# First half of the feed-forward as seven products over halves of K, tokens and gate/up

## The chip, the core and the metric

The kernel runs on one core of one Trainium2 chip. A core has five engines that run side by side, each from its own queue: TensorE (PE, matrix products into PSUM, with its weight loads listed as PEld), VectorE (DVE), ScalarE (ACT), GpSimd (POOL) and SyncE (SP), whose queue here issues the DMAs. The metric is the time on the device in microseconds, from launch to end; smaller is better.

## The reference

Two layers of a diffusion trunk, for 128 context tokens (`x_prompt`) and 1024 latent tokens (`x_sample`) that share one set of weights. Each layer is a mixer (layer 0 latent attention beside gated linear attention, layer 1 differential attention) and a dense SwiGLU feed-forward, each between two RMS norms and scaled by adaLN vectors. All is float32. The change touches the feed-forward and what stands around it:

```python
def trunk_layer(x, li, cond, P, rope, ctx):
    mod = (jax.nn.silu(cond) @ P['w_mod'][li] + P['b_mod'][li])[:, None, :]
    shift1, scale1, gate1, shift2, scale2, gate2 = jnp.split(mod, 6, axis=-1)
    g = P['g_norm'][li]
    ...
    x = x + gate1 * rms_norm(out, g[1])
    h = rms_norm(x, g[2]) * (1.0 + scale2) + shift2
    gate, up = jnp.split(h @ P['w_ffn_in'][li], 2, axis=-1)
    f = (jax.nn.silu(gate) * up) @ P['w_ffn_out'][li]
    x = x + gate2 * rms_norm(f, g[3])
```

The model width is 1024, the hidden width 2816, so `w_ffn_in` is 1024 x 5632 (gate columns, then up columns) and `w_ffn_out` 2816 x 1024.

## The kernel before

**Order.** The program isn't written in the order in which it runs. A `Recorder` (line 171) takes down every operation with its data dependences, and `schedule` (line 327) places them by a list schedule: a cost model gives each operation a duration, and an engine takes the ready operation that can start first, among several the one recorded first. Operations recorded with `copy`, `tt` or `scaled` (lines 635 to 650) may go to one of two or three engines, and the schedule chooses. `issue` (line 504) then emits the operations in that order, each engine working through its own in sequence. All instructions are emitted at line 539, so the profile tells them apart by tile, not by line.

**Memory.** SBUF is cut into named blocks (lines 587 to 591: nine `bU` of 12 KB a partition, four `bW` of 9, six `bE` of 4.5, four `bC` of 3, one `bH` of 9, two `bst` of 4), and tile classes are lists of slots in these blocks (lines 593 to 616). A slot can be given to a tile of one class only when no earlier recorded tile of another class that shares the block is still to be placed. The profile names a tile by its block (U, W, E, C, H, st).

**Products.** A float32 operand is split into a high part, rounded to the type that TensorE takes at full rate (`F32R`), and a remainder, and a product is three matmuls: high by high, high by remainder, remainder by high (`mm3`, line 807).

**First half of the feed-forward** (`ffn_in`, line 1530). The normed input h lies in SBUF transposed, in three groups of 384 tokens (`groups`, line 1367), high parts and remainders. For each of 22 hidden tiles of 128, `load_w` fetches a gate and an up weight (1024 x 128 each) and splits them; for each group `dense_m` makes the two products, ScalarE takes Silu of the gate and VectorE multiplies by the up. The result goes to DRAM (`hid_d`), and for each pair of tiles four sums of token halves go to `hs_d`.

**Second half, and the mixers' output projections** (`project`, line 1428). These are already Strassen products of Winograd's form over latent tokens: seven products of 512 columns ("12", "11", S2, S1, S3, "22", S4 on the left), each looping over pairs j of K tiles: 11 for `w_ffn_out`, 4 for the mixers' outputs. Rows of weights stay in classes `Wr1`, `Wr2` or `Wo`; left operands come from DRAM through class `Ss`; split operands stand in class `k4`.

**Between them** (`finish`, line 1370). `fin(t, parts)` takes a finished block of 128 tokens: norm, gate, add to x, store; and, where another sub-layer follows, the next norm, eight transposes, the adaLN scale and shift, and the split into h. It takes three tiles of 4 KB a partition per block from class `fx`, which has five slots. Block 0 is the context's; it is finished after the second product, blocks 5 to 8 after X and Y are complete, 1 to 4 after the last product.

**adaLN vectors** (`mod_vectors`, line 753). Ten of the twelve vector sets are made on VectorE, 8 passes a set, 80 in all. A pass loads four tiles of `w_mod` (class `M`, two slots), multiplies and adds them into a tile `ma`, transposes and reduces. `beside(n, after)` (line 947) records the next n passes at that point, ready once the operation `after` is done. Before the change 26 are recorded in layer 0's input projections and the rest in layer 0's `ffn_in`, three for each hidden tile until none is left. `diff_qk` (line 1595) makes layer 1's queries and keys from h, tile by tile, and turns them by rotary tables.

## Time and profile before

| | before |
|---|---|
| median of 3 runs | 3533.42 us (3529.42 to 3538.25) |
| the profiled execution's own time | 3530.54 us |
| its span, first to last instruction | 3528.7 us |
| mean granted TensorE clock | 0.967 |
| busy: TensorE, VectorE, ScalarE, GpSimd | 94%, 64%, 38%, 26% of the span |
| moved by DMA | 480.98 MB, 136 GB/s |

Busy time is an average over stages with different limits, so the tables of stretches further down say more than these shares. In the lists of instructions a row gives start, duration, engine, operation, output tile and input tiles, shapes, how many were merged, and in brackets the idle time before it and what ended that. Matmuls are pipelined: the records of two in a row overlap, so the cost of one in a run is the run's length by its count, not a record's own length.

### The profile page before, as it was taken

The page shows a single profiled execution, that of the slowest core. Times are in us where ns is not written, and L with a number is a line of the kernel's source. Part 1 is how long each engine was busy: PE and PEld are TensorE (multiplying, and loading weights), DVE is VectorE, ACT ScalarE, POOL GpSimd, SP SyncE. Part 2 cuts the span into 40 slices and gives each one's busy share as a digit, 9 for nine tenths or more (in the row PEclk, how much of TensorE's full clock was granted, in tenths as well). Part 3 has the DMA queues.
Part 4 walks back from the last instruction along what each step waited for, and adds up shares of the span by engine and source line. Part 5 has one row for each costly group of instructions (what it writes and reads, how often), then busy time and mean ns, then how long its engine had stood idle before and what let it go on. Part 6 is the DMA issues. An engine that isn't in the chain of part 4 may idle for free.

```text
span 3528.7 us, 52056 instructions
## 1 busy us (share of the span) xinstructions
PE 3325.8 (94%) x18525; PEld 3018.3 (86%) x18525; DVE 2256.5 (64%) x5656; ACT 1332.9 (38%) x2558; POOL 933.3 (26%) x858
## 2 busy tenths in 40 slices
...
GB/s 198 141 183 168 170 158 186 109 121 127 151 155 133 161 140 135 147 176 97 90 136 167 198 123 135 139 142 144 78 144 149 105 94 80 99 80 144 109 87 156
DMA packets 433345, 480.98 MB, mean 136 GB/s; under 512 B 38463, under 2 KB 343166, under 8 KB 432414
## 3 DMA queue, kind: packets, MB, share of 16 engines
...
## 4 chain that ended last, share of the span: by engine, by line
PE 53%; DVE 7%; DMA 6%; POOL 3%; issue 2%; ACT 1%; SPq 0%; DVEq 0%; POOLq 0%; ACTq 0%
PE psum L539 53%; DMA M<-in_w_mod 3%; DVE ma L539 2%; POOL E L539 2%; DMA U<-v_d 1%; DVE U L539 1%; DVE E L539 1%; POOL sm L539 1%; ACT E L539 1%; DVE W L539 0%; DVE H L539 0%; DMA U<-in_w_ffn_out 0%; DMA U<-k_d 0%; ACT U L539 0%; DVE C L539 0%
## 5 line engine op out<-in xcount | busy, mean ns | idle before, releaser
L539 PE MATMUL psum<-U,W 128*128 128x384 f32 (+1 forms) x7674 | 1369.9, 337 | 19.8 <-ACT U L539 12.0
L539 PEld LDWEIGHTS psum<-U,W 128*128 128x128 f32 x7674 | 1334.6, 189 | 30.7 <-ACT U L539 13.4
L539 PE MATMUL psum<-E,E 128*128 128x512 f32 x2520 | 589.1, 393 | 17.6 <-DVE E L539 8.4
L539 PEld LDWEIGHTS psum<-E,E 128*128 128x128 f32 x2520 | 470.2, 188 | 129.1 <-DVE E L539 20.3
L539 ACT ACTIVATE E<-psum 128x384 f32<-128x384 f32 (+4 forms) x197 | 98.9, 504 | 944.7 <-PE psum L539 938.1
L539 DVE SCALAR_TENSOR_TENSOR ma<-M,sc,ma 128x128 f32<-128x128 f32 x1120 | 345.3, 372 | 102.6 <-DMA M<-in_w_mod 101.7
L539 PE MATMUL psum<-U,U 128*128 128x384 f32 (+4 forms) x1630 | 328.1, 341 | 4.4 <-DVE E L539 2.3
L539 ACT ACTIVATE E<-E,sm 128x1152 f32<-128x1152 f32 (+1 forms) x248 | 288.1, 1168 | 114.2 <-DVE sm L539 93.3
L539 DVE TENSOR_SCALAR_CACHE_REDUCE E<-psum 128x384 f32<-128x384 f32 (+1 forms) x600 | 303.8, 541 | 33.0 <-PE psum L539 16.0
L539 PE MATMUL psum<-W,U 128*128 128x256 f32 (+2 forms) x1616 | 311.7, 340 | 11.2 <-DVE W L539 3.1
L539 DVE TENSOR_TENSOR E<-E,psum 128x384 f32<-128x384 f32 (+1 forms) x148 | 82.0, 555 | 353.7 <-PE psum L539 353.5
L539 PEld LDWEIGHTS psum<-W,U 128*128 128x128 f32 x1616 | 258.9, 195 | 44.9 <-DVE W L539 5.0
L539 ACT ACTIVATE E<-C 128x512 fp32r<-128x512 f32 (+1 forms) x303 | 181.8, 628 | 285.7 <-PE psum L539 216.6
L539 PEld LDWEIGHTS psum<-U,U 128*128 128x128 f32 (+1 forms) x1630 | 265.3, 191 | 18.6 <-DVE E L539 10.0
L539 DVE TENSOR_TENSOR E<-C,E 128x512 fp32r<-128x512 f32 (+2 forms) x257 | 201.1, 786 | 117.1 <-ACT E L539 111.6
L539 PE MATMUL psum<-U,H 128*128 128x384 f32 x1368 | 247.1, 335 | 0.0
L539 PEld LDWEIGHTS psum<-U,H 128*128 128x128 f32 x1368 | 237.6, 188 | 0.2
L539 DVE TENSOR_TENSOR W<-st,W 128x1024 fp32r<-128x1024 f32 (+3 forms) x111 | 138.3, 1247 | 114.4 <-ACT W L539 112.7
L539 POOL TENSOR_TENSOR E<-C,E 128x512 fp32r<-128x512 f32 (+2 forms) x102 | 131.2, 1287 | 255.8 <-ACT E L539 186.8
L539 PE MATMUL psum<-ident,E 128*128 128x128 f32 x1241 | 175.2, 280 | 20.3 <-POOL E L539 8.1
L539 POOL TENSOR_TENSOR E<-E,E 128x1152 f32<-128x1152 f32 (+2 forms) x74 | 179.0, 2422 | 52.0 <-ACT E L539 26.7
L539 POOL TENSOR_TENSOR sm<-sm,mhalf 128x1 f32<-128x1 f32 (+2 forms) x124 | 93.3, 754 | 342.7 <-DVE sm L539 335.7
...
## 6 DMA issues: line engine op xcount, KB each, us to landing
...
hs_d<-U SPq DMA_DIRECT2D x88, 256.0 KB, 4.0
C<-hs_d SPq DMA_DIRECT2D x88, 256.0 KB, 2.6
...
C<-hid_d SPq DMA_DIRECT2D x66, 256.0 KB, 2.7
```

Source lines behind the costliest of these rows:

```text
L539: getattr(self.real[e], m)(*[res(a) for a in args], **{n: res(a) for n, a in kw.items()})
```

## The change

`ffn_in` handles two hidden tiles (256 gate and 256 up columns) at a time and takes the latent tokens' product as a 2 x 2 by 2 x 2 block product: weights A[r, c], r gate or up, c the half of K (512 rows each); tokens by half of K and half of the 1024 latent tokens. It is done with seven products ("21", "11", T2, T3, T1, T4, "22"), each of two column tiles, four K tiles and 512 tokens. Products that add up stay in the same PSUM tiles. The context tokens' products are made beside, with the tokens as the stationary operand and 256 weight columns moving.

The token side of the seven products is made once, in `fin`: an object `Halves` takes each finished block f (`put`), splits its halves and their sums to high part and remainder and keeps them in SBUF. Blocks 5 to 8 come first; they are stored in DRAM and read back when block 1 to 4 is finished, since the sums need both. The sub-layer that feeds layer 1's mixer keeps the old groups of 384 tokens (`Groups`).

The slots of `Wo` move, `fin` takes its tiles from `fz` or `fy` where `Halves` is the target, and there are new classes for the kept sums, the weights and the temporaries. The passes of `mod_vectors` are spread anew: 23 in layer 0's `ffn_in`, 12 in the products S2 and S1 of its `project`, the rest in `diff_qk`; a pass's first multiplications are recorded with `scaled`.

```diff
-            ("Wo", inside(bU[6:8] + bU[5:6], 4, 3), None), ("Wr1", inside(bU[0:4], 4, 3), None), ("Wr2", inside(bU[4:8], 4, 3), None),
+            ("Wo", inside(bU[4:7], 4, 3), None), ("Wr1", inside(bU[0:4], 4, 3), None), ("Wr2", inside(bU[4:8], 4, 3), None),
             ("F2", inside(bW[0:3], 2, 4) + inside(bE[5:6], 2, 2), None), ("Ss", [(a, a + 2) for a, _ in bC], None),
-            ("k4", [(a, a + 4) for a, _ in bE[0:5]], None), ("fx", inside(bU[8:9], 4, 3) + inside(bH, 4, 2), None), ("Fs", inside(bU[8:9], 2, 6), None),
+            ("k4", [(a, a + 4) for a, _ in bE[0:5]], None), ("fx", inside(bU[8:9], 4, 3) + inside(bH, 4, 2), None),
+            ("Ta", inside(bU[0:4], 4, 3), None), ("Tb", inside(bU[4:8], 4, 3), None),
+            ("Tc", inside(bH, 4, 2) + inside(bU[8:9], 4, 3) + inside(bst[0:1], 4, 1), None),
+            ("fz", inside(bU[7:9], 4, 3), None), ("fy", [(a, a + 4) for a, _ in bE[0:5]] + inside(bst[1:2], 4, 1), None),
+            ("As", [(a, a + 4) for a, _ in bE], None), ("Wb", inside(bW[0:3], 4, 2), None),
+            ("tq", inside(bW[3:4], 2, 4) + [(a, a + 2) for a, _ in bC] + inside(bst[1:2], 2, 2), None),
...
-                        dve.tensor_scalar(out=acc[:, j], in0=st[:, 0, :], scalar1=s, scalar2=None, op0=ALU.mult)
+                        scaled(acc[:, j], st[:, 0, :], s)
...
-    def groups():
-        return [[R.tile("Uh", [128, KD, GW], F32R) for j in range(2)] for g in range(NG)]
+    class Halves:
+        def __init__(self, name):
+            self.name, self.T, self.hc = name, {}, None
+            self.kept = [dtile([128, KD, 128], f"{name}_{q}") for q in range(4)]
+        def split(self, i, q, src):
+            if i not in self.T:
+                cls = {"22": "Ta", "T3": "Ta", "T1": "Ta", "T4": "Tc"}.get(i, "Tb")
+                self.T[i] = [[R.tile(cls, [128, 2, 512], F32R) for _ in range(2)] for _ in range(2)]
+            c = slice(q * 128, (q + 1) * 128)
+            for kp in range(2):
+                hi, lo = [self.T[i][j][kp][:, :, c] for j in range(2)]
+                part = src[:, 2 * kp:2 * kp + 2]
+                copy(hi, part)
+                tt(lo, part, hi, ALU.subtract)
+        def put(self, t, f):
+            a, b = f[:, 0:4], f[:, 4:8]
+            if t == 0:
+                self.hc = [R.tile("Tc", [128, KD, 128], F32R) for _ in range(2)]
+                copy(self.hc[0], f)
+                tt(self.hc[1], f, self.hc[0], ALU.subtract)
+            elif t > 4:
+                self.split("22", t - 5, b)
+                tt(b, b, a, ALU.subtract)
+                self.split("T3", t - 5, b)
+                sp.dma_start(out=self.kept[t - 5], in_=f)
+            else:
+                q = t - 1
+                o = R.tile("fy", [128, KD, 128])
+                sp.dma_start(out=o, in_=self.kept[q])
+                self.split("21", q, b)
+                self.split("11", q, a)
+                tt(o[:, 4:8], o[:, 4:8], a, ALU.add)
+                self.split("T2", q, o[:, 4:8])
+                tt(o[:, 0:4], o[:, 0:4], a, ALU.subtract)
+                self.split("T1", q, o[:, 0:4])
+                tt(b, b, o[:, 4:8], ALU.subtract)
+                self.split("T4", q, b)
+    class Groups:
+        def __init__(self):
+            self.h = [[R.tile("Uh", [128, KD, GW], F32R) for j in range(2)] for g in range(NG)]
+        def put(self, t, f):
+            g, c0 = divmod(t * 128, GW)
+            hi, lo = [v[:, :, c0:c0 + 128] for v in self.h[g]]
+            copy(hi, f)
+            tt(lo, f, hi, ALU.subtract)
...
-            xt, tm = R.tile("fx", [128, D]), R.tile("fx", [128, D])
+            cls = "fx" if not isinstance(h, Halves) else "fy" if 1 <= t <= 4 else "fz"
+            xt, tm = R.tile(cls, [128, D]), R.tile(cls, [128, D])
...
-            u = R.tile("fx", [128, D])
+            u = R.tile(cls, [128, D])
...
-            g, c0 = divmod(t * 128, GW)
-            hi, lo = h[g][0][:, :, c0:c0 + 128], h[g][1][:, :, c0:c0 + 128]
-            copy(hi, f)
-            tt(lo, f, hi, ALU.subtract)
+            h.put(t, f)
...
+    def project(Wm, src_d, s_d, c1, c2, finisher, mods=False):
...
             for j in range(nj):
+                if mods and j % 2 == 0 and s in ("S1", "S2"):
+                    beside(1, at[0])
...
+                at[0] = len(R.ops) - 1
...
+        Th, hc = h.T, h.hc
+        def split_w(src):
+            out = []
+            for kp in range(2):
+                w = R.tile("Wb", [128, 2, 2, 256], F32R)
+                act.activation(out=w[:, 0], in_=src[:, 2 * kp:2 * kp + 2], func=AF.Copy)
+                tt(w[:, 1], src[:, 2 * kp:2 * kp + 2], w[:, 0], ALU.subtract)
+                out.append(w)
+            return out
+        def product(w, i, acc, first, last=False):
+            on = {} if first else {"skip_group_check": True}
+            hi, lo = Th[i]
+            for u in range(2):
+                c = slice(u * 128, (u + 1) * 128)
+                for k in range(4):
+                    wk, a, b = w[k // 2], hi[k // 2][:, k % 2], lo[k // 2][:, k % 2]
+                    with R.group():
+                        pe.matmul(acc[u], lhsT=wk[:, 0, k % 2, c], rhs=a, start=first and k == 0, stop=False, **on)
+                        pe.matmul(acc[u], lhsT=wk[:, 0, k % 2, c], rhs=b, start=False, stop=False, **on)
+                        pe.matmul(acc[u], lhsT=wk[:, 1, k % 2, c], rhs=a, start=False, stop=k == 3, **on)
+        def context(w, half, out, first):
+            for k in range(4):
+                a, b, wk = hc[0][:, half * 4 + k], hc[1][:, half * 4 + k], w[k // 2]
+                with R.group():
+                    pe.matmul(out, lhsT=a, rhs=wk[:, 0, k % 2], start=first and k == 0, stop=False)
+                    pe.matmul(out, lhsT=b, rhs=wk[:, 0, k % 2], start=False, stop=False)
+                    pe.matmul(out, lhsT=a, rhs=wk[:, 1, k % 2], start=False, stop=not first and k == 3)
+        def two(cls="ps"):
+            return [R.tile(cls, [128, 512]) for _ in range(2)]
         for j in range(NH // 2):
-            hid = []
-            for i in (2 * j, 2 * j + 1):
-                if l == 0:
-                    beside(3, start)
-                f = R.tile("E", [128, T])
-                wg_ = load_w([(0, W1[:, i * 128:(i + 1) * 128])])
-                wu_ = load_w([(0, W1[:, FH + i * 128:FH + (i + 1) * 128])])
-                for g in (2, 0, 1):
-                    pg = dense_m(wg_, h, g)
-                    pu = dense_m(wu_, h, g)
-                    s = slice(g * GW, (g + 1) * GW)
-                    act.activation(out=f[:, s], in_=pg, func=AF.Silu)
-                    dve.tensor_tensor(out=f[:, s], in0=f[:, s], in1=pu, op=ALU.mult)
-                sp.dma_start(out=hid_d[i], in_=f)
-                hid.append(f)
-            s1, s2, s3, s4 = [R.tile("Fs", [128, HT]) for _ in range(4)]
-            tt(s1, hid[0][:, L1], hid[1][:, L1], ALU.add)
-            tt(s3, hid[0][:, L0], hid[0][:, L1], ALU.subtract)
-            tt(s2, s1, hid[0][:, L0], ALU.subtract)
-            tt(s4, hid[1][:, L0], s2, ALU.subtract)
-            for i, s in enumerate((s1, s2, s3, s4)):
-                sp.dma_start(out=hs_d[j][i], in_=s)
+            if l == 0:
+                beside(3 if j == 0 else 2, start)
+            A = {}
+            for r, c in ((0, 1), (0, 0), (1, 0), (1, 1)):
+                A[r, c] = R.tile("As", [128, 4, 256])
+                c0 = r * FH + j * 256
+                sp.dma_start(out=A[r, c], in_=W1[c * 512:(c + 1) * 512, c0:c0 + 256].rearrange("(k p) c -> p k c", p=128))
+            pc = ps_tile()
+            C = two()
+            w = split_w(A[0, 1])
+            product(w, "21", C, True)
+            context(w, 1, pc[:, 0:256], True)
+            c1 = two("tq")
+            for u in range(2):
+                copy(c1[u], C[u])
+            P = two()
+            w = split_w(A[0, 0])
+            product(w, "11", P, True)
+            context(w, 0, pc[:, 0:256], False)
+            for u in range(2):
+                dve.tensor_tensor(out=c1[u], in0=c1[u], in1=P[u], op=ALU.add)
+                act.activation(out=c1[u], in_=c1[u], func=AF.Silu)
+            s1, s2 = R.tile("As", [128, 4, 256]), R.tile("As", [128, 4, 256])
+            tt(s1, A[1, 0], A[1, 1], ALU.add)
+            tt(s2, s1, A[0, 0], ALU.subtract)
+            product(split_w(s2), "T2", P, False)
+            X = two("tq")
+            for u in range(2):
+                copy(X[u], P[u])
+            tt(A[0, 0], A[0, 0], A[1, 0], ALU.subtract)
+            B = two()
+            product(split_w(A[0, 0]), "T3", B, True)
+            product(split_w(s1), "T1", P, False)
+            Y = two("tq")
+            for u in range(2):
+                copy(Y[u], P[u])
+                dve.tensor_tensor(out=Y[u], in0=Y[u], in1=B[u], op=ALU.add)
+            w = split_w(A[1, 1])
+            product(w, "T4", B, False)
+            context(w, 1, pc[:, 256:512], True)
+            context(split_w(A[1, 0]), 0, pc[:, 256:512], False)
+            for u in range(2):
+                dve.tensor_tensor(out=X[u], in0=X[u], in1=B[u], op=ALU.add)
+                tt(X[u], X[u], c1[u], ALU.mult)
+            fc, ft = R.tile("tr", [128, 256]), R.tile("tr", [128, 256])
+            act.activation(out=fc, in_=pc[:, 0:256], func=AF.Silu)
+            dve.tensor_tensor(out=fc, in0=fc, in1=pc[:, 256:512], op=ALU.mult)
+            ps = ps_tile()
+            for u in range(2):
+                pe.transpose(ps[:, u * 128:(u + 1) * 128], fc[:, u * 128:(u + 1) * 128], ident)
+            copy(ft, ps[:, 0:256])
+            for u in range(2):
+                sp.dma_start(out=hid_d[2 * j + u][:, 0:NCTX], in_=ft[:, u * 128:(u + 1) * 128])
+            tt(A[0, 1], A[0, 1], s2, ALU.subtract)
+            product(split_w(A[0, 1]), "22", P, False)
+            for u in range(2):
+                g = R.tile("tq", [128, 512])
+                act.activation(out=g, in_=P[u], func=AF.Silu)
+                tt(Y[u], Y[u], g, ALU.mult)
+            sp.dma_start(out=hid_d[2 * j][:, L0], in_=X[0])
+            sp.dma_start(out=hid_d[2 * j + 1][:, L0], in_=X[1])
+            sp.dma_start(out=hid_d[2 * j + 1][:, L1], in_=Y[1])
+            t3 = R.tile("tq", [128, 512])
+            tt(t3, X[0], Y[0], ALU.subtract)
+            tt(Y[0], Y[0], Y[1], ALU.add)
+            t2 = R.tile("tq", [128, 512])
+            tt(t2, Y[0], X[0], ALU.subtract)
+            t4 = R.tile("tq", [128, 512])
+            tt(t4, X[1], t2, ALU.subtract)
+            for i, t in enumerate((Y[0], t2, t3, t4)):
+                sp.dma_start(out=hs_d[j][i], in_=t)
         return hid_d, hs_d
...
-    h = groups()
+    h = Halves("ha")
     project(I["ab_w_out"], mix_d, ms_d, "Wo", "Wo", finish(0, 0, x_in, x_d[0], h))
     hid_d, hs_d = ffn_in(h, 0)
-    h = groups()
-    project(I["w_ffn_out"][0], hid_d, hs_d, "Wr1", "Wr2", finish(0, 1, x_d[0], x_d[1], h))
+    h = Groups()
+    project(I["w_ffn_out"][0], hid_d, hs_d, "Wr1", "Wr2", finish(0, 1, x_d[0], x_d[1], h), True)
+    h = h.h
...
+        beside(2 if m in (0, 1, 8, 9) else 1, len(R.ops) - 1)
...
-    h = groups()
+    h = Halves("hb")
```

3 lines of the change are left out of this document (1 added, 2 removed).

## The prediction

> **What bounds the kernel now.** I read the page first, then the busy time by stretch, then the list of instructions around each seam between stretches.
>
> ```profile
> span 3528.7 us, 52056 instructions
> PE 3325.8 (94%) x18525; PEld 3018.3 (86%) x18525; DVE 2256.5 (64%) x5656; ACT 1332.9 (38%) x2558; POOL 933.3 (26%) x858
> ...
> PE 53%; DVE 7%; DMA 6%; POOL 3%; issue 2%; ACT 1%; SPq 0%; DVEq 0%; POOLq 0%; ACTq 0%
> ```
>
> TensorE is busy 94% of the span and holds 53% of the chain that ended last, no other engine more than 7%. But that is an average over stages, so here are five stretches. Columns: stretch, length, busy time of each engine with its instructions, granted clock, DMA share, GB/s.
>
> ```profile
> 1008.00:1553.00 545.00, 533.41 (x3135) 529.24 (x3134) 403.93 (x1138) 73.58 (x109) 53.61 (x30) 0.99 0.45 140
> 1655.00:1735.00 80.00, 78.99 (x344) 62.24 (x343) 50.23 (x65) 38.42 (x69) 37.95 (x28) 1.00 0.36 108
> 1950.00:2147.00 197.00, 197.00 (x1142) 196.74 (x1141) 139.14 (x338) 38.35 (x85) 25.55 (x20) 1.00 0.51 156
> 2660.00:2713.00 53.00, 22.20 (x104) 19.78 (x104) 39.88 (x73) 29.73 (x71) 10.89 (x15) 0.65 0.46 156
> 2750.00:3200.00 450.00, 450.00 (x2598) 450.00 (x2597) 91.93 (x108) 62.95 (x91) 31.03 (x18) 1.00 0.27 88
> ```
>
> In order: the first half of layer 0's feed-forward, with the adaLN passes of `mod_vectors` beside it; layer 0's output projection (mostly products S2 and S1); `diff_qk`; the seam ahead of layer 1's first half; and that first half itself. The last row is the purest: TensorE busy 450 of 450 us at clock 1.00, VectorE 92, ScalarE 63. There only fewer or cheaper matmuls help. It gives 450/2598 = 0.1732 us per 384-column matmul. The seam is the opposite, with TensorE busy 22 of 53 us at a mean clock of 0.65: what follows the last product sets it. In layer 0's projection VectorE and GpSimd already work 50 and 38 of 80 us under a full TensorE.
>
> **The matmuls.** The code of before runs 2 x 2 x 3 x 8 x 3 = 288 matmuls of 384 columns per pair of hidden tiles. The change runs 7 products of 2 x 4 x 3 = 168 matmuls of 512 columns, 4 x 4 x 3 = 48 of 256 for the context tokens, and 2 transposes. Prices of both widths stand in unbroken runs:
>
> ```profile
> 1682.71 77.62 PE L539 MATMUL psum<-E,E 128*128 128x512 f32 x339 [0.41 <-DVE E L539]
> 714.74 2.48 PE L539 MATMUL psum<-W,U 128*128 128x256 f32 x20
> 2659.02 1.03 PE L539 MATMUL psum<-ident,H 128*128 128x128 f32 x8
> ```
>
> 512 columns: 77.62/339 = 0.229 us. 256 columns: 2.48/20 = 0.124, and less the drain of the last, which overlaps when more follows, some 0.116; I take 0.12. A transpose is 1.03/8 = 0.13. Before: 288 x 0.1732 = 49.9 us a pair. After: 168 x 0.229 + 48 x 0.12 + 2 x 0.13 = 38.5 + 5.8 + 0.3 = 44.5. The gain is 5.4 us in each of 22 pairs, **-118 us**, if TensorE stays fed.
>
> **Can the others feed it?**
>
> ```profile
> L539 ACT ACTIVATE E<-C 128x512 fp32r<-128x512 f32 x300 | 180.2, 629 | 283.5 <-PE psum L539 216.6 <-DVE E L539 12.9 <-DVE U L539 11.7
> L539 DVE TENSOR_TENSOR E<-C,E 128x512 fp32r<-128x512 f32 x208 | 175.0, 845 | 115.5 <-ACT E L539 111.6
> L539 DVE TENSOR_TENSOR E<-psum,E 128x512 fp32r<-128x512 f32 x28 | 19.2, 689 | 46.7 <-ACT E L539 46.6
> L539 DVE TENSOR_TENSOR W<-st,W 128x1024 fp32r<-128x1024 f32 x102 | 132.9, 1303 | 111.2 <-ACT W L539 109.6 <-DMA M<-in_w_mod 1.0
> L539 POOL TENSOR_TENSOR E<-C,E 128x512 fp32r<-128x512 f32 x92 | 125.5, 1365 | 197.2 <-ACT E L539 185.5 <-issue 8.2 <-POOL E L539 2.0
> ```
>
> A pair now splits eight weight sets instead of four loads: 16 remainders of 512 columns, four weight sums of 1024, six additions from PSUM, four products and four token sums of 512. At 0.69 us (third row, whose operand comes from PSUM) and 1.30 that is 30 x 0.69 + 4 x 1.3 = 26 us of VectorE in 44.5, GpSimd taking some. ScalarE has 16 splits, 6 copies and 4 Silus at 0.63, so 16 us. In layer 1 both fit under TensorE. Between products TensorE must wait until an accumulator is read: the second product's sums are read before the third adds to the same bank. One read (0.69) runs under the other bank's 12 matmuls (2.75 us), so the cover is large; I take **+5 us** for jitter. If that cover went, three handovers a pair at about 1 us would cost 66.
>
> **The seams into the first half.** The last product ends at 2659, and then the normalised rows of tiles 5 to 8 and 1 to 4 are finished, one after another:
>
> ```profile
> 2648.13 1.27 DVE L539 TENSOR_TENSOR E<-E,psum 128x512 f32<-128x512 f32 x2
> ...
> 2668.86 1.97 PE L539 MATMUL psum<-ident,H 128*128 128x128 f32 x8 [8.80 <-DVE H L539]
> 2677.45 1.94 PE L539 MATMUL psum<-ident,U 128*128 128x128 f32 x8 [6.62 <-DVE U L539]
> 2686.25 1.97 PE L539 MATMUL psum<-ident,U 128*128 128x128 f32 x8 [6.86 <-ACT U L539]
> 2691.85 0.69 PE L539 MATMUL psum<-U,W 128*128 128x384 f32 x1 [3.63 <-ACT U L539]
> ...
> 2695.83 1.43 PE L539 MATMUL psum<-ident,H 128*128 128x128 f32 x8
> ...
> 2703.35 1.04 PE L539 MATMUL psum<-ident,U 128*128 128x128 f32 x8
> ...
> 2711.90 1.91 PE L539 MATMUL psum<-ident,U 128*128 128x128 f32 x8
> ```
>
> The sums of X and Y start at 2648.13. Each group of eight transposes, that at 2659.02 above the first, is one tile; the spacing is 8.7 us. FFN matmuls begin at 2691.85, when tiles 6 to 8 (group 2) are ready. The stretch from 2660 to 2713 has 104 instructions, 48 of them transposes, so 56 FFN matmuls (9.7 us of work) slip in before TensorE is full; that equals a full start at 2703. After the change the first product, "21", needs all four tiles 1 to 4, the last to be finished. Their `put` also grows: ten copies and ten remainders of 256 columns and three sums of 512, where one copy and one remainder of 1024 stood.
>
> ```profile
> L539 DVE TENSOR_TENSOR C<-C,C 128x256 f32<-128x256 f32 x15 | 6.7, 443 | 0.6
> 2673.88 0.69 DVE L539 CAST U<-H 128x1024 fp32r<-128x1024 f32 x1
> 2674.61 1.22 DVE L539 TENSOR_TENSOR U<-H,U 128x1024 fp32r<-128x1024 f32 x1
> ```
>
> On VectorE that is 10 x 0.44 + 3 x 0.69 = 6.5 us against 1.2, with the copies on ScalarE; tiles 5 to 8 grow by 4 x 0.44 + 0.69 - 1.2 = 1.2 us. Against it, `fz` and `fy` have six slots each where `fx` had five for three tiles a token block, so two blocks can overlap. VectorE is busy 39.9 us for six tiles in the seam, 6.6 each. Floor: 6.6 us a tile for all, ScalarE and GpSimd taking what `put` adds, so "21" starts at 2659 + 7 x 6.6 + 4 = 2709. Ceiling: 8.7 and, for the last four, 8.7 + 5.3 = 14: 2659 + 26 + 56 + 4 = 2745. I take 7 and 9 us, nearest the busy time plus what `put` adds: 2659 + 21 + 36 + 4 = 2720. The context matmuls of two weight sets (24 x 0.12 = 2.9 us) can run ahead, so 2717: 14 us later than 2703, twice: **+28 us** (6 to 78). The four tiles that `put` stores and reads back per layer (512 KB each) are read at least three blocks after their store; I count them at nothing. Uncovered, at twice the 2.7 us of the 256 KB row below, they would cost 5 us a block, 40 in all.
>
> **The seams out of it.**
>
> ```profile
> 3224.68 29.28 PE L539 MATMUL psum<-U,W 128*128 128x384 f32 x168
> 3253.80 6.56 PE L539 MATMUL psum<-E,E 128*128 128x512 f32 x25
> ...
> C<-hid_d SPq DMA_DIRECT2D x66, 256.0 KB, 2.7
> ```
>
> Today the projection follows without a gap, its first left operand having been loaded before. Now its staging class `Ss` shares the blocks of `tq`, and a slot is given only once every earlier `tq` tile is placed; the last, t4, is placed after the last product's Silu (0.63), product, sum and t2 (3 x 0.69), near 3.5 us with hand-offs. Then come load (2.7), high part (0.63) and remainder (0.69), near 8 us in all: **+16 us** for two (12 to 24).
>
> **The adaLN passes.** 80 passes exist; 26 run earlier, and of the 54 now in layer 0's first half 31 move: 12 into S2 and S1 of its output projection, 19 into `diff_qk`.
>
> ```profile
> 1210.21 1.66 DVE L539 SCALAR_TENSOR_TENSOR ma<-M,sc,ma 128x128 f32<-128x128 f32 x6
> L539 DVE SCALAR_TENSOR_TENSOR ma<-M,sc,ma 128x128 f32<-128x128 f32 x1120 | 345.3, 372 | 102.6 <-DMA M<-in_w_mod 101.7
> L539 DVE STREAM_TRANSPOSE S<-ma 128x256 f32<-128x256 f32 x80 | 35.5, 443 | 1.8
> L539 DVE TENSOR_REDUCE mt<-S 128x8 f32<-128x256 f32 x80 | 33.4, 417 | 2.1
> L539 POOL TENSOR_TENSOR C<-C,C 128x384 f32<-128x384 f32 x22 | 31.8, 1446 | 103.3 <-DVE C L539 61.9 <-ACT W L539 21.2 <-DMA q_d<-E 10.6
> L539 DVE TENSOR_TENSOR C<-C,E 128x384 f32<-128x384 f32 x63 | 31.9, 548 | 0.0
> L539 DVE CAST E<-C 128x384 fp32r<-128x384 f32 x39 | 14.1, 360 | 11.3 <-POOL C L539 9.9 <-DMA q_d<-E 0.3
> ```
>
> A pass is 16 multiply-adds at 1.66/6 = 0.28, a transpose and a reduction (0.44 + 0.42): 5.3 us of VectorE. Its waits for weight rows are 102.6 us for 80 passes, 1.3 each: 6.6 us. Its four loads (124 in all) move in SP's queue too, ahead of `Ss` loads, and wait there for the two M slots; SP can issue nothing behind them meanwhile. That the first multiplication may go to other engines I count as nothing.
>
> - Projection: S2 takes four 512-column operations and 2.75 us of TensorE per step, S1 three. Passes come today no further than 545/54 = 10 us apart; none takes under 6.6. At 10, VectorE has 4.7 us left, six or seven operations, and GpSimd at 1.37 does seven: 3.5 steps, about what TensorE does, no loss. At 6.6 VectorE has nothing left and GpSimd does 4.8 operations: in S2's six passes (40 us) 7 of 11 steps, in S1's nearly 10, +34 in all. Between them, at 8 us, S2 loses 6, with the waits not filled 15 and S1 4. I take **+12** (0 to 34).
> - `diff_qk`: VectorE 139 + 19 x 6.6 = 264 in 197 us, 67 too many. GpSimd has 171 free, 118 operations at 1.446 that VectorE does in 0.55, so 65; copies to ScalarE free 14. It just fits; **+8** (0 to 67).
> - Layer 0's first half: its stretch of 545 us has 3135 instructions, some 108 of them the small sums of passes (8 for four); 3027 x 0.1732 = 524, so it loses 21 us today. VectorE's load falls there from about 54 us a pair (six passes, 12 gated products, splits) to 26 + 13 = 39: **-8** (-18 to 0).
>
> **Sum.** -118 + 5 + 28 + 16 + 12 + 8 - 8 = -57 us. The profiled execution took 3530.5 us (span 3528.7 plus 1.8 around it): 3473.5. The median of the runs shown is 2.9 above it, so I predict **3476 us** against 3533.4.
>
> **Rivals.**
> 1. *GpSimd is no help, and the moved passes lie open.* Slower. The rows for it:
>
> ```profile
> 2651.50 1.79 POOL L539 TENSOR_TENSOR E<-U,E 128x512 fp32r<-128x512 f32 x1
> 2652.06 1.78 DVE L539 TENSOR_TENSOR E<-C,E 128x512 fp32r<-128x512 f32 x1
> 2653.76 0.68 DVE L539 TENSOR_TENSOR U<-U 128x512 f32<-128x512 f32 x1
> ```
>
> A 512-column remainder that takes VectorE 0.69 alone took 1.78 beside a GpSimd one. If all were so, S2 needs 44 x 0.69 + 6 x 6.6 = 70 us, S1 33 x 0.69 + 40 = 62, each against 30: +72; `diff_qk` some +64. That is 136 where I carry 20: 3476 + 116 = **3592**. Without these two stages the sum is -77: from 77 us lost there it is slower. Against it: the mean of such remainders is 0.845, not 1.78, and the 80 us stretch of the projection had both engines busy 50 and 38 us with TensorE at 79. The Trainium skill, page "SBUF — State Buffer", section "SBUF: two separate sides", states this rule: the port pair that VectorE and GpSimd share is an exclusive lock for a whole instruction, also for a VectorE operation with two SBUF inputs. The pair of rows agrees; the mean says that they meet seldom.
> 2. *The seams cost their ceilings.* 78 + 24 instead of 28 + 16: 3476 + 58 = **3534**, no change. For it: ten small splits a tile on a VectorE that is already busy 75% of the seam. Against: more slots, ScalarE and GpSimd half idle.
> 3. *Nearly all hides.* Seams 6 and 12, passes 0, handovers 0, layer 0 -18: 3533 - 118 = **3415**. Against: the load of the projection and `diff_qk`.
>
> That the matmuls aren't saved can't be: the program fixes their count.
>
> **Chances.** My forecast (3435 to 3515) 0.53, the first rival 0.13, the second 0.20, the third 0.14. The range 3425 to 3545 takes in the second and the upper part of the third, and leaves out the first. Runs of this kernel spread by 0.25%, so 0.3%, 10.6 us, is about what a measurement can tell from no change. Faster by more: 0.53 + 0.14 + a quarter of the second = 0.72; slower: 0.13 + 0.03 = 0.16; within: 0.12.
>
> **What would show it.** Layer 1's first half should fill TensorE in about 490 us where it took some 550; matmuls of "21" should start near 2717 on today's time scale; a gap near 8 us should stand ahead of the projections; and S2 should last about 40 us instead of 30, with VectorE near full. I am wrong if TensorE shows gaps inside layer 1's pairs, if 512-column matmuls take other than 0.229 there, or if `diff_qk` lengthens by tens of us.

## The result, and the profile after

The changed kernel is slower: **3634.26 us** (3633.99 to 3634.79, three runs) against 3533.42, a ratio of 1.0285 (95% interval 1.0261 to 1.0308). The forecast was 3476 with a range of 3425 to 3545. The page of the changed kernel, in the rows that were shown of before:

```profile
span 3633.0 us, 50899 instructions
...
PE 3251.6 (90%) x16985; PEld 2780.4 (77%) x16985; DVE 2643.9 (73%) x5930; ACT 1595.0 (44%) x3136; POOL 1188.2 (33%) x1088
...
PE 42%; DVE 13%; issue 7%; POOL 4%; DMA 4%; ACT 2%; SPq 0%; POOLq 0%; DVEq 0%; ACTq 0%
```

TensorE has 1540 matmuls fewer and is busy 74 us less, yet the span grew by 104 us. VectorE gained 387 busy us and nearly doubled its share of the chain that ended last, from 7% to 13%. So TensorE now stands still some 180 us longer. Where it waits is read from the same table of stretches: stretch, length, busy time of TensorE, its weight loads, VectorE, ScalarE and GpSimd with their instructions, granted clock, DMA share, GB/s.

```profile
1013.00:1557.00 544.00, 505.07 (x2433) 423.98 (x2433) 408.19 (x699) 183.69 (x330) 132.23 (x96) 0.96 0.36 116
1690.00:1770.00 80.00, 60.44 (x230) 45.60 (x228) 77.42 (x142) 26.82 (x52) 43.75 (x32) 0.82 0.35 101
2012.00:2266.00 254.00, 215.63 (x1194) 212.81 (x1193) 236.81 (x552) 55.02 (x132) 107.64 (x107) 0.93 0.54 162
2785.00:2856.00 71.00, 17.52 (x75) 14.32 (x73) 66.68 (x132) 41.43 (x104) 38.72 (x39) 0.56 0.51 179
2900.00:3300.00 400.00, 400.00 (x1974) 339.06 (x1973) 232.03 (x300) 147.29 (x255) 41.21 (x19) 1.00 0.28 93
```

In the order of the rows: layer 0's first half with 23 adaLN passes beside it; its output projection; `diff_qk`; the seam ahead of layer 1's first half; that first half. The second row holds the later half of the product S2, all of S1 and the start of S3. The last row is as forecast: TensorE is full, at clock 1.00. In the projection it is busy 60 of 80 us where it was busy 79 of 80, with VectorE at 77 of 80. In `diff_qk` the stretch itself is 254 us instead of 201, and VectorE is busy in 93% of it.

For a whole account the span is cut at the matmuls that begin and end each stage in TensorE's list (first and last matmul of the kind; us):

| stage | before | after | difference |
|---|---|---|---|
| last mixer product to first FFN product, layer 0 | 32.0 | 70.4 | +38.4 |
| first half, layer 0 | 584.2 | 542.8 | -41.4 |
| to the projection, layer 0 | 0 | 13.5 | +13.5 |
| projection, layer 0 | 257.4 | 316.8 | +59.4 |
| `diff_qk` | 200.9 | 254.0 | +53.1 |
| from there to the mixer's last product, layer 1 | 512.3 | 518.2 | +5.9 |
| last mixer product to first FFN product, layer 1 | 32.7 | 71.2 | +38.5 |
| first half, layer 1 | 562.1 | 488.2 | -73.9 |
| to the projection, layer 1 | 0 | 13.3 | +13.3 |

These sum to 107, the other stages to -3. In layer 1, where no pass stands beside it, seam, first half and the gap to the projection fell together from 594.8 to 572.7, by 22 us: the new product form does pay. In layer 0 the same three rows grew by 10, and 112 us were lost in two stages that the product form does not touch. The theory that the experiments were made for (A): **the moved passes made the loss**. Its rivals: the products and seams made it (B), or only both together (C).

### The profile page after: what moved, and what is told of

It is laid out like the page before. It is cut to its first block, busy times and chain, and to the rows that moved or that the text cites. A ratio compares the mean times of both kernels' runs of the same rounds, so it can differ in the third digit from the quotient of the medians.

```text
span 3633.0 us, 50899 instructions
## 1 busy us (share of the span) xinstructions
PE 3251.6 (90%) x16985; PEld 2780.4 (77%) x16985; DVE 2643.9 (73%) x5930; ACT 1595.0 (44%) x3136; POOL 1188.2 (33%) x1088
## 4 chain that ended last, share of the span: by engine, by line
PE 42%; DVE 13%; issue 7%; POOL 4%; DMA 4%; ACT 2%; SPq 0%; POOLq 0%; DVEq 0%; ACTq 0%
PE psum L539 42%; DVE ma L539 5%; DVE E L539 3%; POOL E L539 2%; DMA M<-in_w_mod 2%; DVE U L539 2%; DVE C L539 1%; DVE W L539 1%; ACT E L539 1%; POOL sm L539 1%; DMA U<-v_d 1%; DMA C<-hid_d 1%; DVE H L539 0%; POOL st L539 0%; POOL U L539 0%
## 5 line engine op out<-in xcount | busy, mean ns | idle before, releaser
L539 PE MATMUL psum<-U,W 128*128 128x512 f32 (+1 forms) x6010 | 1314.4, 374 | 14.4 <-DVE W L539 6.3
L539 PEld LDWEIGHTS psum<-U,W 128*128 128x128 f32 x6010 | 1105.3, 192 | 161.4 <-issue 14.5
L539 POOL TENSOR_TENSOR E<-E,E 128x1152 f32<-128x1152 f32 (+4 forms) x110 | 265.3, 2414 | 632.6 <-DVE W L539 543.6
L539 DVE TENSOR_TENSOR W<-E,W 128x512 fp32r<-128x512 f32 x327 | 262.6, 807 | 195.8 <-ACT W L539 193.2
L539 ACT ACTIVATE E<-C 128x512 fp32r<-128x512 f32 (+2 forms) x326 | 191.5, 613 | 377.3 <-PE psum L539 238.8
L539 ACT ACTIVATE W<-E 128x512 fp32r<-128x512 f32 x352 | 220.5, 628 | 277.1 <-PE psum L539 215.6
L539 ACT ACTIVATE E<-E,sm 128x1152 f32<-128x1152 f32 (+2 forms) x254 | 294.6, 1168 | 107.1 <-DVE sm L539 86.9
L539 PE MATMUL psum<-W,U 128*128 128x256 f32 (+1 forms) x1616 | 311.7, 339 | 10.8 <-DVE W L539 3.5
L539 ACT ACTIVATE W<-psum 128x384 fp32r<-128x384 f32 (+2 forms) x381 | 183.3, 513 | 125.6 <-PE psum L539 123.4
L539 PEld LDWEIGHTS psum<-ident,E 128*128 128x128 f32 x1273 | 150.6, 146 | 64.2 <-DVE E L539 18.6
```

The costliest lines, as they stand in the source:

```text
L539: getattr(self.real[e], m)(*[res(a) for a in args], **{n: res(a) for n, a in kw.items()})
```

## The experiments

Times are medians. A ratio is to runs of the kernel before on the same chip, with its 95% interval; without an interval there was one run. Stages are cut as above: first half and projection of layer 0, `diff_qk`, from there to layer 1's last mixer product, the seam and the first half of layer 1.

| kernel | us | ratio | half 0 | proj. 0 | `diff_qk` | to mixer's end | seam 1 | half 1 |
|---|---|---|---|---|---|---|---|---|
| before | 3533 | | 584 | 257 | 201 | 512 | 33 | 562 |
| after | 3634 | 1.0285 (1.0261 to 1.0308) | 543 | 317 | 254 | 518 | 71 | 488 |
| a1_no_passes | 3471 | 0.9812 (0.9773 to 0.9852) | 488 | 257 | 201 | 514 | 70 | 488 |
| b1_no_passes | 3534 | 0.9993 (0.9982 to 1.0005) | 564 | 258 | 201 | 515 | 33 | 563 |
| b2_passes_moved | 3644 | 1.0300 (1.0262 to 1.0339) | 567 | 318 | 255 | 523 | 34 | 563 |
| a2_own_bank | 3631 | 1.0264 (1.0226 to 1.0301) | 542 | 310 | 255 | 520 | 71 | 488 |
| a3_no_gpsimd | 3620 | 1.0243 | 539 | 297 | 255 | 520 | 71 | 488 |
| a4_on_tensor | 3617 | 1.0226 (1.0210 to 1.0242) | 575 | 279 | 249 | 513 | 69 | 488 |
| a5_psum_sum | 3630 | 1.0266 | 542 | 317 | 227 | 537 | 69 | 488 |
| a6_short_put | 3622 | 1.0244 | 543 | 318 | 255 | 519 | 62 | 486 |
| a10_slots | 3592 | 1.0163 (1.0145 to 1.0180) | 567 | 280 | 249 | 512 | 69 | 487 |
| c2_late_sums | 3577 | 1.0123 (1.0103 to 1.0144) | 522 | 309 | 250 | 519 | 70 | 489 |
| c7_late_psum_qk | 3597 | 1.0174 (1.0153 to 1.0194) | 531 | 313 | 229 | 539 | 69 | 490 |
| c9_late_psum_all | 3570 | 1.0102 (1.0080 to 1.0123) | 504 | 313 | 229 | 541 | 69 | 490 |
| u1_back | 3599 | 1.0173 (1.0152 to 1.0193) | 621 | 260 | 201 | 517 | 69 | 490 |
| d2_places_only | 3564 | 1.0073 (1.0049 to 1.0096) | 556 | 258 | 222 | 519 | 71 | 491 |
| c10_places | 3502 | 0.9909 (0.9891 to 0.9928) | 514 | 260 | 230 | 510 | 70 | 495 |
| c11_places_sbuf_qk | 3532 | 0.9990 (0.9979 to 1.0001) | 512 | 259 | 249 | 515 | 71 | 493 |
| c12_places_more | 3490 | 0.9873 (0.9854 to 0.9891) | 525 | 261 | 204 | 512 | 69 | 495 |

### Which of the two changes lost the time

By the reduction that ends a pass, the groups of VectorE in the kernel before, ahead of 1008 us and from there on, count 25 passes and 55, one more than the 54 of my prediction:

```profile
L539 DVE TENSOR_REDUCE mt<-S 128x8 f32<-128x256 f32 x25 | 10.4, 417 | 0.6
...
L539 DVE TENSOR_REDUCE mt<-S 128x8 f32<-128x256 f32 x55 | 23.0, 417 | 1.5
```

a1 (after) and b1 (before) leave out these 55 and one earlier pass, and put constants in their place; b2 is the kernel before with the passes at the places that they have after.

```diff
-    later = itertools.chain(*(mod_vectors(l, c) for l, c in ((0, 2), (0, 4), (0, 3), (0, 5), (1, 1), (1, 0), (1, 2),
-                                                             (1, 4), (1, 3), (1, 5))))
+    later = itertools.chain(*(mod_vectors(l, c) for l, c in ((0, 2), (0, 4), (0, 3))))
+    for l, c in ((0, 5), (1, 1), (1, 0), (1, 2), (1, 4), (1, 3), (1, 5)):
+        pool.memset(mod[l][:, c], 0.0 if c in (0, 3) else 1.0)
```

> The changed kernel with the last seven adaLN vector sets (56 of the 80 passes) left out and replaced by constants. Theory A, the moved passes made the loss: the output projection of layer 0 falls from 316 to about 245 us and the stage of layer 1's queries and keys from 254 to about 197, and layer 0's first half of the feed-forward from 543 to about 495, so 3634 becomes about 3460. Rival B, the seven products and their seams made it: those three stages barely move, and the time stays above 3580.

> The kernel before with the same seven sets left out. Its first half in layer 0 loses its 21 us of waits and no more: about 3510. By theory A the changed kernel without passes is then faster than this one by the matmuls less the seams, -118 + 2 x 27 + 2 x 12 = some 40 us; by rival B it is slower.

> The kernel before with only the passes moved to where the change puts them (23 in layer 0's first half, 12 in S2 and S1 of its projection, 19 with layer 1's queries and keys). Theory A: the projection and the queries and keys lose the same 72 and 57 us as in the changed kernel, less the 21 us that the first half regains: about 3640. Rival C, the passes hurt only together with the new first half (its stores, its buffers): within 15 us of 3533.

Theory A held. Without passes the two forms differ by the product form alone: seam, first half and gap are 22 us shorter in layer 0 and 24 in layer 1 (a1 against b1), where the expectation said 40 for both together. Without passes the new form takes 488, 257 and 201 us in the three stages; the passes cost 55, 60 and 53 there, 168 together. In the kernel before they cost 584 - 564 = 20. (b1's whole time, 3534 where 3510 was expected, doesn't show these 20, since its order of instructions came out 25 us longer ahead of layer 0's first half.) The move alone, in the old form, costs 61 + 54 in the two stages less 17 in the first half: b2 is as slow as the change.

Then why did the 55 passes cost only 20 where they stood? A stretch of layer 0's first half without them in the old form (b1), and then that of the new form with one of its projection (a1):

```profile
1030.00:1560.00 530.00, 530.00 (x3062) 529.97 (x3062) 112.06 (x137) 74.64 (x110) 33.61 (x20) 1.00 0.28 93
```

```profile
1025.00:1505.00 480.00, 476.93 (x2341) 403.88 (x2341) 277.27 (x359) 177.10 (x306) 52.03 (x23) 1.00 0.31 104
1525.00:1780.00 255.00, 252.90 (x1038) 192.60 (x1037) 145.34 (x200) 106.05 (x190) 84.85 (x64) 0.99 0.34 103
```

In the first half VectorE's own work rose from 21% of the stretch to 58%. The old form left 418 us free in 530, the new one 203 in 480. u1 tests this: the passes go back.

```diff
-                beside(3 if j == 0 else 2, start)
+                beside(6, start)
```

> The kernel after with its passes put back, all 54 into layer 0's first half (six a pair until none is left), nothing else changed. At 2.4 us for each, as 23 of them cost there, the first half takes 488 + 130 = 618 us, the projection 257 and diff_qk 201, the whole 3471 + 130 = 3601. Theory A in its strong form (the move itself made the loss): the whole falls to 3560 or below. Rival U (the new first half has no room for them as the old one had, so that the move only spread a loss): 3585 to 3660.

Rival U held. The first half takes 621 us (618 expected), 133 more than without passes, and 54 of the 55 passes end in it; the projection and `diff_qk` are whole again. So the move was no free choice: the new form uses up the room that the passes had, and, made as they are, they cost well over 100 us in either place. This is why undoing the move alone wins back 36 us, a fifth of the 168.

### Why a pass costs so much

A pass has 5.3 us of VectorE work. Layer 0's projection leaves VectorE 110 of 255 us (second row of a1), and twelve passes at 5.3 are 64; yet they cost 60. TensorE's list, cut where each product begins, shows in which products (us):

| kernel | S2 and S1 | S3 | other four | projection |
|---|---|---|---|---|
| before | 62.7 | 29.9 | 164.8 | 257.4 |
| a1_no_passes | 62.7 | 29.9 | 164.2 | 256.8 |
| after | 85.8 | 66.4 | 164.6 | 316.8 |
| a3_no_gpsimd | 84.9 | 47.2 | 164.6 | 296.7 |
| a2_own_bank | 85.7 | 52.0 | 171.7 | 309.5 |
| c2_late_sums | 86.2 | 49.6 | 173.5 | 309.2 |
| c9_late_psum_all | 68.5 | 78.3 | 166.1 | 312.9 |

So 23 of the 60 us are lost in S2 and S1, where the passes are recorded, and 36 in S3 behind them: only five of the twelve passes end in S2 and S1, and six in S3. In S1, the changed kernel's VectorE list shows the same multiply-adds at two speeds:

```profile
1739.87 3.17 DVE L539 SCALAR_TENSOR_TENSOR ma<-M,sc,ma 128x128 f32<-128x128 f32 x4
...
1743.56 1.13 DVE L539 SCALAR_TENSOR_TENSOR ma<-M,sc,ma 128x128 f32<-128x128 f32 x4
```

And GpSimd's list at that time:

```profile
1739.66 2.70 POOL L539 TENSOR_TENSOR E<-C,E 128x512 fp32r<-128x512 f32 x2 [0.73 <-ACT E L539]
1745.37 1.30 POOL L539 TENSOR_TENSOR E<-C,E 128x512 fp32r<-128x512 f32 x1 [3.01 <-ACT E L539]
```

Four take 1.13 us while GpSimd is idle, and 3.17 beside two GpSimd operations of 2.70 us together. By the starts and ends of all records of the projection, the 44 of the 168 multiply-adds that overlap a GpSimd operation have a mean length of 1.04 us, and the other 124 have 0.34. (Records in a row overlap here, so four of 0.34 take 1.13.) TensorE then stands before what VectorE is late with. Its waits in the projection, by operand, in total with the longest last, and the one entry in its list:

```profile
PE psum L539 <- DVE mt L539: 27.1, 2, 26.7
PE psum L539 <- DVE E L539: 16.5, 9, 4.3
PE psum L539 <- ACT E L539: 14.1, 2, 11.7
```

```profile
1795.40 0.30 PE L539 MATMUL psum<-mt,quarter 128*32 128x8 f32 x8 [26.69 <-DVE mt L539]
```

Eight matmul records of 0.30 us together, the small sums of four passes, hold TensorE for 26.7 us: they stand in its order ahead of most of S3's products. SyncE's list at that time, and the busy time of the engines in these 26.7 us:

```profile
1765.66 25.77 SPq L539 DMA_DIRECT2D M<-in_w_mod  x16
```

```profile
1768.70:1795.40 26.70, 0.01 (x2) 0.00 (x0) 19.66 (x66) 1.22 (x4) 1.19 (x4) 0.50 0.25 73
```

VectorE works through the last four passes there, 6.7 us each, beside a GpSimd that is busy for 1.2 us, while SyncE issues their 16 loads of weight rows and no left operand. These four passes are not slowed by GpSimd; they are late, and TensorE stands in line behind them. Two candidates then for the loss, the shutting out (a5, a3) and the order (a2, c2); that the weight rows' loads cost the time by themselves is a third, which a4 below tests. In a5 the multiply-adds of `diff_qk` read the running sum from PSUM:

```diff
+            run = R.tile("S1", [128, 512])[:, 0:256].rearrange("p (a b) -> p a b", a=2) if late else acc
...
-                        scaled(acc[:, j], st[:, 0, :], s)
+                        dve.tensor_scalar(out=run[:, j], in0=st[:, 0, :], scalar1=s, scalar2=None, op0=ALU.mult)
...
-                        stt(acc[:, j], st[:, k % 2, :], s, acc[:, j], ALU.mult, ALU.add)
+                        stt(acc[:, j] if k == KD - 1 else run[:, j], st[:, k % 2, :], s, run[:, j], ALU.mult, ALU.add)
```

> The kernel after; in diff_qk alone a pass keeps its running sum in PSUM, so that a multiply-add of VectorE reads one operand from SBUF and one from PSUM. Theory K (VectorE's multiply-adds with two SBUF inputs shut out GpSimd and are shut out by it): in the stretch of diff_qk their mean falls from 0.536 to 0.27-0.36 us, GpSimd's sums of 128x384 get shorter too, and diff_qk takes 215 to 235 us where it took 254. Rival L (it is plain throughput, or the waits for rows): the mean stays above 0.45 us or the stretch stays at 248 to 258 us.

In a3, S1 and S2 keep their sums from GpSimd:

```diff
-        R.either(("dve", "pool"), "tensor_tensor", out=out, in0=in0, in1=in1, op=op)
+        R.either(("dve",) if now.get("dve") else ("dve", "pool"), "tensor_tensor", out=out, in0=in0, in1=in1, op=op)
```

> The kernel after; in S2 and S1 of layer 0's projection the sums and remainders may go to VectorE alone and not to GpSimd. Theory K (shutting out): the mean of a multiply-add of a pass falls in that stage from about 0.5 to 0.28-0.33 us, and the projection stays within 15 us of 317 although VectorE does GpSimd's share as well. Rival L (GpSimd's help is real): the mean stays above 0.42 us, and the projection takes 340 us or more.

The groups of these multiply-adds (count, busy time, mean ns, waits before them): after, in the projection and in `diff_qk`:

```profile
L539 DVE SCALAR_TENSOR_TENSOR ma<-M,sc,ma 128x128 f32<-128x128 f32 x168 | 78.8, 526 | 9.3 <-DMA M<-in_w_mod 6.6 <-POOL ma L539 2.3
...
L539 DVE SCALAR_TENSOR_TENSOR ma<-M,sc,ma 128x128 f32<-128x128 f32 x266 | 126.2, 536 | 4.3 <-DMA M<-in_w_mod 3.0 <-POOL ma L539 0.7 <-ACT ma L539 0.5
```

a3 in the projection, and a5 in `diff_qk`:

```profile
L539 DVE SCALAR_TENSOR_TENSOR ma<-M,sc,ma 128x128 f32<-128x128 f32 x168 | 53.2, 376 | 4.5 <-DMA M<-in_w_mod 2.9 <-POOL ma L539 1.3
```

```profile
L539 DVE SCALAR_TENSOR_TENSOR psum<-M,sc,psum 128x128 f32<-128x128 f32 x192 | 66.6, 347 | 6.7 <-DMA M<-in_w_mod 5.7
```

Theory K held in kind: 526 became 376, a little over the range named, and 536 became 347. With the sum in PSUM the 82 of a5's 224 multiply-adds there (the row has 192, the last of each sum stand apart) that overlap a GpSimd operation are as long as the others, 0.34 and 0.35 us. This agrees with the Trainium skill, page "SBUF — State Buffer", section "SBUF: two separate sides": a VectorE operation with two SBUF inputs and a GpSimd operation that reads SBUF exclude each other for a whole instruction. The projection got 20 us *shorter* although VectorE took GpSimd's share of two products. By the table of products S2 and S1 took 85 us as before, but eight passes ended in them and not five; the 20 us came in S3, which had three passes left and not six. So GpSimd's help was a loss there. `diff_qk` fell by 27 us to 227, but the stage behind it grew by 19 and the part ahead of layer 0's first half by 7, so a5 as a whole gained 4. Four passes end in the stage behind `diff_qk` in a5, and one in the changed kernel; that this is the cause was not tried by itself.

For the order, a2 gives the small sums a PSUM class of their own, and c2 records them one pass later (with a second `mt` slot, and a10's change of slots, below):

```diff
+    R.add_class("pm", "PSUM", [(b, b + 1) for b in range(7, -1, -1)], None)
...
-                mod_finish(l, c, m - 3, 4, ps)
+                    mod_finish(l, c, m - 3, 4, ps)
...
+                    held.append((made[0], small))
```

> The changed kernel with one edit: the tile for the sums of four passes takes its PSUM bank from a class of its own, so that it no longer stands in line ahead of the eight banks of the projection. Theory D: the 26.7 us in which TensorE waits ahead of S3 came from that line, and the time falls by about 27 to 3607. Rival E: VectorE was too slow with the passes anyway, the wait turns up elsewhere in the projection, and the time stays within 8 us of 3634.

> The kernel after with the slots of tq changed as in a10_slots, and the small sums of the passes (the matmuls on mt and what follows them) recorded one pass later, with two mt slots and a PSUM class of their own. Theory P (a good part of the passes' cost is TensorE standing in order before a small sum that VectorE hasn't finished: 22.7, 27.1 and 14.9 us of waits for mt in the three stages): these waits fall under 10 us together, the three stages (543 + 317 + 254) by 35 to 65 us, the whole from 3634 by that and the 27 us of the slots to 3542-3572. Rival Q (VectorE is late by so much, and the wait only turns up at another operand): the three stages fall by less than 15 us, the whole is 3592 to 3610.

The bank mattered little (-3): rival E held. In a2's projection the wait for `mt` fell from 27.1 to 3.2 us, but waits for other sums that VectorE is late with grew from 16.5 to 26.6. c2's whole is just above its theory's range: it lost 57 us, 27 of them by the slots, and the three stages fell by 21 + 8 + 4 = 33, between the two ranges. The wait for `mt` is gone in the first half (22.7 to nothing) and in the projection (27.1), but in the projection the waits for other sums grew to 28.4 us, and in `diff_qk` those for `mt` grew from 14.9 to 22.8. So the order is a part in the first half, and mostly a symptom elsewhere.

c7 and c9 join the two cures: PSUM sums in `diff_qk`, then in all three stages.

> c2_late_sums with the running sum of the passes of diff_qk in PSUM, as in a5_psum_sum. Theory K (VectorE's operations with two SBUF inputs and GpSimd's shut each other out): diff_qk falls to 215-232 us, and the whole by 10 to 30 against c2_late_sums. Rival: what diff_qk gains, the attention behind it loses, as in a5_psum_sum, and the whole is within 8 us of c2_late_sums.

> c7_late_psum_qk with the running sums in PSUM in layer 0's first half and its output projection too, from a bank of the class ps. Theory K: the mean of a pass's multiply-add falls from 0.48 to 0.27-0.35 us there also, layer 0's first half to 495-520 and the projection to 265-290, the whole to 3490-3545. Rival S (the bank is missed by the products, or it is VectorE's load and not the shutting out): the two stages together fall by less than 15 us against c7_late_psum_qk or rise.

Of c7's theory the stage held and the whole did not: `diff_qk` gained 21, the stage behind lost 21, as the rival said, and the whole got longer by 20, since its order of instructions also came out 11 us longer ahead of layer 0's first half and 9 longer in it. c9's whole, 3570, misses its theory's range too. It brought the first half to 504, so a pass costs 0.7 us there, and S2 and S1 from 86 to 68.5 us, with four passes ending in them where five did. But the projection stayed at 313: seven passes end in S3, and TensorE lost 44.4 us there in two waits that a pass's last multiply-add ended, the one that gives back the bank of its running sum.

The last way to do without VectorE is TensorE itself:

```diff
+                            pe.matmul(ps[:, 0:2], lhsT=st[:, i, :], rhs=sc[:, k + i, :],
+                                      start=k + i == 0, stop=k + i == KD - 1)
```

> The kernel after with the last seven of its ten adaLN sets (56 of 80 passes) made at the same places, from the same loads, as small matmuls on TensorE (the block of the weight stationary, two columns moving), with a PSUM class of their own, and not on VectorE. Theory A (what the moved passes cost is VectorE's time: their multiply-adds delay the operations that feed TensorE): layer 0's first half falls from 543 to 490-500 us, its projection from 317 to 257-270, diff_qk from 254 to 201-215; the whole is 3471 (no passes at all) plus TensorE's own time for 448 matmuls of two columns, 3475 to 3520. Rival F (their cost is the weight rows: loads in SP's queue and waits for two M slots, which stay as they were, and TensorE now waits for them itself): the projection stays above 290 and diff_qk above 235, the whole 3560 to 3650.

The whole and `diff_qk` came out in F's ranges, but not by F's reason. The projection fell to 279 and `diff_qk` to 249: the passes took 23.3 and 37.6 us of TensorE there, and it waited only 0.7 and 6.3 us for weight rows. So the rows' loads, which stayed, cost little in these two stages; what was lost there came of the passes' work on VectorE. The first half rose to 575. Its groups on TensorE show why:

```profile
L539 PE MATMUL psum<-sc,M 128*128 128x2 f32 x368 | 49.3, 254 | 22.1 <-DMA M<-in_w_mod 21.7
```

The 23 passes are 184 matmuls of two columns here, which the list shows as two records each: 49.3 us of TensorE (2.1 a pass, where the expectation had at most 49/56 = 0.9), and 21.7 us of waits for weight rows. In this stage VectorE is the cheaper place: 55 us in the changed kernel, 87 in a4.

### Seams

a6 shortens `put`, a10 changes slots on top of a4:

```diff
-                self.split("T2", q, o[:, 4:8])
-                tt(o[:, 0:4], o[:, 0:4], a, ALU.subtract)
-                self.split("T1", q, o[:, 0:4])
-                tt(b, b, o[:, 4:8], ALU.subtract)
-                self.split("T4", q, b)
+                self.T["T2"], self.T["T1"], self.T["T4"] = self.T["21"], self.T["11"], self.T["21"]
```

```diff
-            ("tq", inside(bW[3:4], 2, 4) + [(a, a + 2) for a, _ in bC] + inside(bst[1:2], 2, 2), None),
+            ("tq", inside(bW[3:4], 2, 4) + [(a, a + 2) for a, _ in bC[0:2]] + inside(bst[1:2], 2, 2), None),
```

> The kernel after; put leaves out, for blocks 1 to 4, the three sums and the six high parts and remainders of T2, T1 and T4; their products read the tiles of 21 and 11 instead, so the products and their count are the same. Theory M (put's work on VectorE and GpSimd sets the end of the seam): the stretch from the last product to the first product of the feed-forward falls from 71 to 45-58 us in both layers, the whole by 26 to 50. Rival N (the chain of the blocks through fin, with its slots, transposes and hand-offs, sets it): the stretch stays at 64 to 72 us, the whole within 14 us of the kernel after.

> a4_on_tensor with two changes of slots: tq gives up the last of its three bC blocks' slots, so that a slot of Ss is free of tq at the end of the first half, and fy gets two more slots. Theory G (the gap of 13.5 us ahead of each projection is the chain from t4 to the first Ss load, because Ss shares blocks with tq): both gaps fall to under 4 us, the whole is 18 to 28 us below a4_on_tensor. Rival H (the gap is the write of hs_d and its read back, or the hidden rows' own dependence, whatever the slot): the gaps stay above 10 us and the whole is within 8 us of a4_on_tensor. If more fy slots help, the stretch ahead of the first half falls from 71 us by 5 or more in both layers; otherwise it stays within 3 us.

TensorE's list in the changed kernel's seam of layer 1, from the last product's end to the first product "21":

```profile
2784.55 1.03 PE L539 MATMUL psum<-ident,U 128*128 128x128 f32 x8
2792.77 1.97 PE L539 MATMUL psum<-ident,U 128*128 128x128 f32 x8 [7.19 <-DVE U L539]
...
2816.72 1.91 PE L539 MATMUL psum<-ident,U 128*128 128x128 f32 x8
...
2824.13 1.97 PE L539 MATMUL psum<-ident,st 128*128 128x128 f32 x8 [3.57 <-DVE st L539]
2837.04 1.97 PE L539 MATMUL psum<-ident,st 128*128 128x128 f32 x8 [10.95 <-ACT st L539]
2851.67 1.97 PE L539 MATMUL psum<-ident,E 128*128 128x128 f32 x8 [12.66 <-DVE E L539]
2855.88 0.77 PE L539 MATMUL psum<-U,W 128*128 128x512 f32 x1 [2.24 <-DVE U L539]
```

The last two tiles come 13 and 15 us behind the one before, and VectorE is busy 66.7 of the 71 us (table of stretches above). a6 took off 9 us in each layer, between its theory's 13 to 26 and its rival's 0 to 7, and 12 of the whole, as the rival said. So what a6 leaves out of `put` accounts for 9 us; how the rest divides between the other splits and the chain through `fin` was not tried. The two more slots of `fy` in a10 changed nothing (69.2 against a4's 69.0).

At the other end theory G held without rest. After, and then a10:

```profile
3343.96 1.95 PE L539 MATMUL psum<-ident,mod 128*128 128x128 f32 x16
3357.39 22.97 PE L539 MATMUL psum<-E,E 128*128 128x512 f32 x88 [11.48 <-ACT E L539]
```

```profile
3304.64 4.34 PE L539 MATMUL psum<-U,W 128*128 128x512 f32 x18
3308.82 11.04 PE L539 MATMUL psum<-E,E 128*128 128x512 f32 x48
```

The gap is gone, 13.3 us twice, from one block whose slot `tq` no longer claims, and a10's whole is 25 us below a4's.

### Places

Where do the 55 passes cost least? c10 has 33 in layer 0's first half, 14 in `diff_qk` and 8 in layer 1's first half (the set used last), in the manner of c9; c11 is c10 with SBUF sums in `diff_qk`; c12 has 42, 5 and 8; d2 has c12's places in the manner of the changed kernel. The edit of d2:

```diff
-                beside(3 if j == 0 else 2, start)
+                beside(4 if j < 9 else 3, start)
+            elif j < 8:
+                beside(1, start)
...
-    project(I["w_ffn_out"][0], hid_d, hs_d, "Wr1", "Wr2", finish(0, 1, x_d[0], x_d[1], h), True)
+    project(I["w_ffn_out"][0], hid_d, hs_d, "Wr1", "Wr2", finish(0, 1, x_d[0], x_d[1], h))
...
-        beside(2 if m in (0, 1, 8, 9) else 1, len(R.ops) - 1)
+        beside(1 if m in (0, 1, 2, 8, 9) else 0, len(R.ops) - 1)
```

> c9_late_psum_all with the passes at other places: 33 in layer 0's first half (three a pair), none in its output projection, 13 in diff_qk, the last eight in layer 1's first half. Theory A (the place decides: the two stages of TensorE at 490 us have VectorE to spare, the projection hasn't): the projection falls from 313 to 257-262, diff_qk and the attention together from 770 to 735-760, layer 0's first half stays at 505-520, layer 1's at 490-500; the whole 3480 to 3530. Rival T (the stages of the seven products have no more room than the projection): the first halves rise by 2 us or more for each pass put there (layer 0 over 525, layer 1 over 505), and the whole stays above 3540.

> c10_places with the running sum in SBUF in diff_qk alone. If the gain of PSUM sums in diff_qk goes back into the attention, as in a5_psum_sum and c7_late_psum_qk: within 10 us of c10_places, with diff_qk longer by 8 to 20 us and the attention shorter by as much. Otherwise slower by 10 or more.

> c10_places with 42 passes in layer 0's first half (four a pair), 4 in diff_qk, 8 in layer 1's first half. Theory A: VectorE's work in layer 0's first half is then 26 us of the pair's own and some 20 of passes in 44.5, so it is at its limit: that stage 515 to 550, diff_qk 203 to 212, the whole within 20 us of c10_places on either side. Rival T: the first half above 550.

> The kernel after with the passes at the places of c12_places_more (42 in layer 0's first half, 4 in diff_qk, 8 in layer 1's first half), nothing else changed: sums in SBUF, small sums in order, tq as it was. If the place gives most of it: the whole is c12's 3490 plus the 27 us of the slots plus at most 25, 3517 to 3542. If the manner gives most of it (each pass still costs 2.4 us in a first half): 3471 + 50 x 2.4 + 4 x 2.8 = 3602, so 3580 to 3620.

Theory A (the place decides) held in all its ranges, in c10 and in c12, and both are faster than the kernel before, though by little: c10 by 0.9%, and c12 by 1.3%, at 3490 us, a ratio of 0.9873 (0.9854 to 0.9891). Its three stretches (both first halves, and `diff_qk` between them), and behind them the first stretch in d2:

```profile
1025.00:1525.00 500.00, 474.75 (x2329) 395.28 (x2328) 445.35 (x991) 170.94 (x296) 138.72 (x83) 0.98 0.42 133
1960.00:2150.00 190.00, 184.75 (x1059) 181.62 (x1058) 149.88 (x399) 40.63 (x91) 46.93 (x45) 1.00 0.57 166
2750.00:3200.00 450.00, 448.43 (x2212) 377.86 (x2213) 290.85 (x459) 165.21 (x285) 46.65 (x20) 1.00 0.34 112
```

```profile
1025.00:1525.00 500.00, 453.46 (x2204) 372.50 (x2203) 453.03 (x931) 170.88 (x314) 158.41 (x119) 0.98 0.39 121
```

VectorE works 445 of 500 us in layer 0's first half, and TensorE still 475. Of c12's 42 passes 39 end in that stage and three in the projection, and they cost 525 - 488 = 37 us in the one and 4 in the other: 1.0 each, where the changed kernel pays 55/23 = 2.4. In layer 1's first half 8 passes cost 7 us. In d2 VectorE is about as busy in the same stretch, 453 us, but TensorE does less, 453, and the 42 passes cost 68, or 1.6 each. So at about the same load the manner of a pass changes what it costs. d2, at 3564, lies between its two ranges: of the 144 us from the changed kernel to c12 the places alone give 70, the slots 27 (the two gaps), and the manner of a pass the other 47, if the three simply add up. In c11 the gain did not go back into the attention: PSUM sums in `diff_qk` were worth 30 us, 19 of them in that stage, 5 in the stage behind it and 4 ahead of layer 0's first half. The stage behind is 20 us longer only where four passes end in it (a5, c7, c9); why they cost so much there was not tried by itself.

## Why the prediction was wrong

By its own steps, with what the runs give (us):

| step | predicted | measured |
|---|---|---|
| matmuls and handovers | -113 | -122 |
| seams into the first halves | +28 (6 to 78) | +49 |
| seams out | +16 (12 to 24) | +27 |
| passes: projection, `diff_qk`, layer 0's half | +12 | +148 |
| sum | -57 | +102 |

The spans differ by 104.

- **Matmuls and handovers: right.** The first half of layer 1 was to fill TensorE in about 490 us; it took 488.2, and in layer 0 without passes 487.8. Before, at the quoted 49.9 us a pair, eleven pairs are 549, so each layer gained 61. Of the 5 us set aside for handovers nothing was needed.
- **Seams in: the mechanism right, the size small.** From last to first product it is 38.5 us more in layer 1. Before, 13 us of the first half were lost while only part of the tokens was ready (562 - 549), and 15 in layer 0 (564 without passes): 25 and 23 net. I had taken 9 us a tile for the last four; the last ones came 13 and 15 us apart, about the 14 that I had named as the ceiling.
- **Seams out: right in kind**, 13.4 for 8. That `Ss` waits for the last `tq` tile was the cause, as a10 shows.
- **The passes: wrong, and the difference comes from this step.** I wrote +12 for the projection, +8 for `diff_qk` and -8 for layer 0's first half. They are +60, +53 and +35 (55 now, 20 before). Four reasons failed together:
  - The passes were costed at 0.28 us a multiply-add, the price beside an idle GpSimd; by busy time and count it is 0.47 in the two stages (78.8/168 and 126.2/266).
  - GpSimd was counted as help ("GpSimd has 171 free"): a3 shows that in S2 and S1 it takes away more than it gives: without it they are as long, and three passes more end in them.
  - Only S2 and S1 were counted in the projection. They grew by 23 us, within the 0 to 34 that I had allowed. The other 36 are in S3, for which I had no term, although twelve passes at my own 6.6 us need 79 us and I had put the two products at 60 + 12.
  - I took VectorE's 26 + 13 us in 44.5 a pair for room enough in layer 0's first half. The load was counted rightly (26 of 44.5 is the 58% of a1), but with the 23 passes (408 of 544, 75%) TensorE already waits: a pass costs 2.4 us there (23 in the changed kernel, 54 in u1), where it had cost 20/55 = 0.4. The load alone does not set this price: c12 pays 1.0 a pass with VectorE at 89%.

My first rival had the shutting out, and nearly the size: 136 us in the two stages, where 113 were measured, a forecast of 3592. For `diff_qk` (64 against 53) it was right; for the projection the nearness is luck, since it put 72 us into S2 and S1, which lost 23, and had nothing for S3. I gave it 0.13, on the mean of remainders (0.845 and not 1.78), which said that the two engines meet seldom. That mean came from a kernel whose projection keeps VectorE busy 50 of 80 us. With the passes beside the same work it is busy 77 of 80, and 44 of 168 multiply-adds met a GpSimd operation, where 21 of 770 had in layer 0's first half before: the mean belongs to the load that it was measured under. Of the signs that I had named, layer 1's pairs without gaps and an S2 of 41 us, with VectorE near full, spoke for the forecast, and `diff_qk` longer by tens of us against it, before any experiment.
